# A two-layer trunk on one core: norm weight of v moved into v's stage, wider pairs, mixing over both token tiles at once

## The chip, the cores and the metric

The kernel runs on one core of a Trainium2 chip. The metric is the device time of one execution in microseconds, the median of several runs. The engines are named as in the profile: PE (TensorE, matmuls; PEld are its weight loads), DVE (VectorE), ACT (ScalarE), POOL (GpSimd) and SP (SyncE, which here issues DMAs only).

## The reference, cut to what matters

There are 256 tokens (two token tiles of 128) of width 2048 and two layers. The change touches the first layer, a gated MLP with mixing over positions, and the first projection of the second, attention.

```python
def gmlp_branch(xn, w_in, v_g, w_s, b_s, w_out):      # W = 4096
    proj = xn @ w_in                                  # [u | v | gate], 3 x 4096 columns
    uv = gelu(proj[..., :2 * W]);  zg = proj[..., 2 * W:]
    u, v = split(uv)
    v = rms_norm(v, v_g)                              # over 4096, times v_g
    vc = v.reshape(B, S // 128, 128, 16, 256)         # 16 groups of 256 columns
    mixed = einsum('gts,bnsgc->bntgc', tril(w_s), vc) + b_s
    y = u * mixed * silu(zg)
    return y @ w_out

def stick_breaking_branch(xn, w_in, w_out):
    q, k, v, zg = split(xn @ w_in, 4)                 # 4 x 2048 columns
    o = stick_breaking_attention(q, k, v) * silu(zg)
    return o @ w_out

h = x
h = h + gmlp_branch(rms_norm(h, norm_g[0]), ...)
h = h + stick_breaking_branch(rms_norm(h, norm_g[1]), ...)
return rms_norm(h, final_g)
```

All inputs are float32. All weights are streamed from memory in every execution.

## The kernel before

**Products in three terms.** A float32 tile is split into a high part (`hi`, a rounded copy that ACT makes, line 114) and the rest (`lo`, a subtraction on DVE, line 115); `cut` does this for weights, two tiles of 128x512 at a time. `terms` (lines 119 to 121) adds hi x hi, hi x lo and lo x hi in a PSUM bank. Each is one matmul of 512 columns.

**Pairs.** The class `Pair` makes two blocks of 512 output columns for both token tiles. For `ks` tile pairs (rows k and k+4 of the inner dimension, then 8 and 9 as the fifth) it uses seven products in place of eight: blocks p1 to p7 with sums and differences of the weight tiles (`minus` and the addition, DVE, lines 275 and 300; `plus`, an accumulating DMA that POOL issues, line 280) and of the left operand (`Left.sums`, and `Left.fifth` for the fifth pair of tiles, whose scratch are the buffers `sg0` and `sg1`). Every other k tile (`rest`) goes the plain way in `column(0)` and `column(1)`, one step for two k tiles, 12 matmuls. `head` makes p1 and p5, `body` p6, p2, p7, p3 and p4, then calls `mid` and makes column 0. Column 1 of a pair runs in between the blocks of the next one (`run`). A pair with `ks` = 5 has a third group of one tile in each block; where its tile is put is told by the argument `fifth`.

**Stages.** After a first plain pair, v is made in three pairs (v2, v4, v6, each with `KS_A` = 4); `evac_v` writes gelu(v) to SBUF and sums its squares. Then eight u/gate pairs (gu0 to gu7, `KS_GU` = 4), each for 512 columns of gate (column 0) and of u (column 1). Their `mid_gu` calls `mixing`: load v's norm weight (`vg`) and the mixing matrices (`ws`) on POOL's queue, mask and split `ws`, scale and split v (`vh`, `vl`), and for each token tile and group three matmuls of 256 columns (lines 580 to 582). DVE multiplies the result from PSUM by `vg` into `ym` (line 584). `evac_gu` then adds the bias and multiplies by silu(gate) (line 595, one instruction for each of the two groups) and, after u's gelu, multiplies by it (line 600). The output projection of the layer follows (pairs o0 and o2, plain products), then the first q/k pair (qk0, with `ks` = 4; the later ones, and v and gate of the attention, have 5), whose head runs beside the tail of o2.

**What sets the order.** The kernel is traced in the order of the program; small pieces of work are put in `queue` and are started by `tick`, one after so many blocks or steps. A scheduler orders the instructions of each engine by its own estimate of times; the engines then work their queues in this fixed order, with semaphores. Some orders are written out: `issue_after` puts an instruction behind another on its engine; `load` issues on SP. Buffers: three for raw weights of the plain steps (`wraw`), five for the split ones (`wspl`), one each for the tiles of the blocks.

Of the kernel before, what the change touches and what calls it, by code (L numbers as in the profile page):

```python
# [20 lines left out]
KS_GU = 4  # L21
# [8 lines left out]
def trunk_kernel(ctx: ExitStack, tc: tile.TileContext, x, xt, gcols, wst, a_w_in, a_v_norm_g,  # L30
# [188 lines left out]
    def load(out, in_):  # L219

        ins = ins_of(nc.sync.dma_start(out, in_))
        if chain:
            if chain[0] is not None:
                tc.add_manual_dep(ins, chain[0], NOSYNC, reason="order of loads")
            chain[0] = ins.name

    class Pair:
# [3 lines left out]
        def __init__(self, src, left, nk, name, ks, evac, mid=None, fifth=None):  # L231
            self.fifth = fifth or (lambda j, name: ex.tile([P, 1, CB], F32, tag=f"b1{j + 1}_2", name=name))
            self.src, self.left, self.name, self.ks = src, left, name, ks
            self.evac, self.mid = evac, mid
            self.rest = [k for k in range(nk) if k not in HALVES[0][:ks] + HALVES[1][:ks]]
            self.groups = [(k, min(2, ks - k)) for k in range(0, ks, 2)]

        def bank(self, nm):
            return ps_acc.tile([P, CB], F32, tag="acc", name=f"{self.name}_{nm}")

        def load(self, i, j):
            tiles = []
            for g, (k, n) in enumerate(self.groups):
                if i and g >= 2:
                    break
# [5 lines left out]
                load(raw, self.src(HALVES[i][k], n, j))  # L251
                tiles.append(raw)
            return tiles
# [8 lines left out]
        def block(self, b, part, acc, nm, first=False):  # L262

            for g, (k0, n) in enumerate(self.groups):
                hi, lo = cut(b[g], n, f"{self.name}_{nm}{g}")
                for kk in range(n):
                    k = k0 + kk
                    lh, ll = part(k)
                    terms(acc, lh, ll, hi[:, kk, :], lo[:, kk, :], first and k == 0, k == self.ks - 1)
                tick(1)  # L270
                yield

        def minus(self, into, b0, b1):
            for g in range(len(self.groups)):
                nc.vector.tensor_sub(into[g], b0[g], b1[g])  # L275

        def plus(self, into, i, j, g0=0):

            for g, (k, n) in list(enumerate(self.groups))[g0:]:
                adds.append(nc.gpsimd.dma_start(into[g], self.src(HALVES[i][k], n, j), accum_op=ALU.add))  # L280

        def head(self):
# [11 lines left out]
            self.minus(self.b11, self.b12, self.b11)  # L294
# [202 lines left out]
    def v_pair0(b):  # L497
        p = Pair(columns(a_w_in, W + b * CB, W + (b + 1) * CB), left, KD, f"v{b}", KS_A,
                 lambda j, t, bank: evac_v(b + j, t, bank))
        return p  # L500

# [15 lines left out]
    left.sums(max(KS_A, KS_GU), home("xs", [P, 2, 4, max(KS_A, KS_GU), P], F32R, "xs0"), "s0")  # L517
# [23 lines left out]
    l0 = ctx.enter_context(ExitStack())  # L541
    py = l0.enter_context(tc.tile_pool(name="py", bufs=1))

# [3 lines left out]
    with ExitStack() as lg:  # L547
        pa = lg.enter_context(tc.tile_pool(name="pa", bufs=1))
        pb = lg.enter_context(tc.tile_pool(name="pb", bufs=2))
        mixed = {}  # L550
        rv = None

        def mixing(b, pair):

            vg = pa.tile([P, CB], F32, tag="vg", name=f"vg{b}")
# [13 lines left out]
            mixed[b] = []  # L569
            for t in range(NT):  # L570
                vh = pb.tile([P, CB], F32R, tag="vh", name=f"vh{b}_{t}")
                vl = pb.tile([P, CB], F32R, tag="vl", name=f"vl{b}_{t}")
                vs = v_of(t, b * CB, CB)
                nc.scalar.activation(vh, vs, AF.Identity, scale=rv[:, t:t + 1])
                nc.vector.scalar_tensor_tensor(vl, vs, rv[:, t:t + 1], f(vh), op0=ALU.mult, op1=ALU.subtract)
                mp = ps_ms.tile([P, CB], F32, tag="ms", name=f"mix{b}_{t}")
                for j in range(GPB):
                    o = mp[:, j * GD:(j + 1) * GD]
                    sl = slice(j * GD, (j + 1) * GD)
                    nc.tensor.matmul(o, wh[:, j, :], vh[:, sl], start=True, stop=False)  # L580
                    nc.tensor.matmul(o, wh[:, j, :], vl[:, sl], start=False, stop=False)
                    nc.tensor.matmul(o, wl[:, j, :], vh[:, sl], start=False, stop=True)
                ym = pa.tile([P, CB], F32, tag=f"ym{t}", name=f"ym{b}_{t}")
                nc.vector.tensor_mul(ym, mp, vg)
                mixed[b].append(ym)

        def evac_gu(b, j, t, bank):
            ym = mixed[b][t]
            if j == 0:
                sg = jk.tile([P, CB], F32, tag=f"sg{t}", bufs=1, name=f"sg{b}_{t}")  # L590
                nc.scalar.activation(sg, bank, AF.Silu, scale=r1[:, t:t + 1])
                for i in range(GPB):
                    g = b * GPB + i
                    sl = slice(i * GD, (i + 1) * GD)
                    nc.vector.scalar_tensor_tensor(ym[:, sl], ym[:, sl], cols[:, NG + g:NG + g + 1], sg[:, sl],
                                                   op0=ALU.add, op1=ALU.mult)
            else:
                y = v_of(t, b * CB, CB)
                nc.scalar.activation(y, bank, AF.Gelu_apprx_tanh, scale=r1[:, t:t + 1])
                nc.vector.tensor_mul(y, y, ym)  # L600
# [11 lines left out]
        for b in range(NV):  # L612
            run(Pair(columns(a_w_in, 2 * W + b * CB, b * CB), left, KD, f"gu{b}", KS_GU,
                     lambda j, t, bank, b=b: evac_gu(b, j, t, bank), mid=lambda pair, b=b: mid_gu(b, pair)))
        flush()
        prior.clear()

# [92 lines left out]

    def o_pair(c, evac, mid):
        def fifth(j, name):

            return jk.tile([P, 1, CB], F32, tag=f"sg{j}", bufs=1, name=name)
# [67 lines left out]
    for _ in p.head():  # L782
        next(tail)
# [18 lines left out]
    nc.vector.tensor_copy(mones, scr[:, 0, :])  # L802
# [3 lines left out]
    nc.vector.tensor_copy(nu, scr2)  # L806

    never = pd.tile([P, 2, P], BF16, name="never")
    nc.vector.memset(never, 0.0)
# [3 lines left out]
    nc.vector.tensor_copy(one, ident)  # L813
# [342 lines left out]
```

## Time and profile before

| what | value |
|---|---|
| median of 3 runs (lowest, highest) | 1147.48 us (1147.37, 1147.52) |
| profiled execution: time | 1147.16 us |
| its span, from first to last instruction | 1145.4 us |
| PE busy, matmuls | 1134.8 us, 5222 |
| DVE busy | 1006.3 us |
| ACT busy | 816.6 us |
| POOL busy | 94.5 us |
| bytes moved by DMA | 263.69 MB |
| granted clock of PE | 0.998 |

The span is that of the profiled execution; the rest of its time, 1.8 us, lies around it. Times in the rows are microseconds from the span's start, lengths of single instructions in groups are ns. A row of a group gives line, engine and operation, written tile <- read tiles, shape and count, then busy time, mean length, and the idle time of the engine just before, with what ended it. Matmul records overlap, since matmuls are pipelined; the distance of their starts tells what a slot costs. DVE's and ACT's records overlap a little as well.

### The profile page before, as it was taken

How to read it: one execution, taken by the hardware profiler on the slowest of the kernel's cores; microseconds unless marked ns; L12 is line 12 of the kernel's file. 1: busy time of each engine (PE TensorE's matmuls, PEld its weight loads, DVE VectorE, ACT ScalarE, POOL GpSimd, SP SyncE). 2: the span in 40 equal slices, each digit the busy share in tenths (PEclk: the TensorE clock that was granted, in tenths of full speed). 3: DMA queues.
4: the chain of work that ended last, by engine and by line, in shares of the span. 5: the costliest groups of instructions: out<-in, count | busy, mean ns of one | idle time of the engine just before them, and what ended most of it. 6: DMA issues, size and time to landing. Idle time of an engine off the chain costs nothing.

```text
span 1145.4 us, 14888 instructions
## 1 busy us (share of the span) xinstructions
PE 1134.8 (99%) x5222; PEld 940.5 (82%) x5222; DVE 1006.3 (88%) x1108; ACT 816.6 (71%) x1072; POOL 94.5 (8%) x101
## 2 busy tenths in 40 slices
PE   9999999999999999999999999999999999999997
PEld 6788888888888888888888888888888888888885
DVE  7988888998999998987988679989889989897995
ACT  7777767767767767856657456788678877886574
POOL 0200010110110110100010000110100101100000
PEclk9999999999999999999999999999999999999999
DMA  9988787786787786677795768687787876837972
GB/s 330 319 274 250 194 262 256 195 270 231 204 258 241 212 257 224 182 236 203 254 270 171 266 201 284 170 268 208 184 283 199 211 228 173 273 87 241 334 225 82
DMA packets 135020, 263.69 MB, mean 230 GB/s; under 512 B 8864, under 2 KB 9376, under 8 KB 134816
## 3 DMA queue, kind: packets, MB, share of 16 engines
q1 hardware_dynamic: 117408, 227.57, 59.1%
q0 software_dynamic: 15728, 31.99, 15.6%
q10 hardware_dynamic: 1808, 3.17, 0.8%
q8 instruction: 41, 0.67, 0.2%
q14 instruction: 35, 0.29, 0.1%
HBM read 258.50 MB, written 4.19 MB: 229 GB/s over the span
## 4 chain that ended last, share of the span: by engine, by line
PE 96%; DMA 1%; ACT 1%; issue 1%; DVE 1%; SPq 0%; POOLq 0%; POOL 0%; ACTq 0%
PE gu_a L121 3%; PE gu_a L120 3%; PE gu_b L121 3%; PE gu_a L119 3%; PE gu_b L120 3%; PE gu_b L119 3%; PE gu_d L121 2%; PE op_acc L121 2%; PE gu_d L120 2%; PE op_acc L119 2%; PE op_acc L120 2%; PE gu_c L121 2%; PE gu_d L119 2%; PE gu_c L120 2%; PE gu_c L119 2%; PE qk_a L121 1%
## 5 line engine op out<-in xcount | busy, mean ns | idle before, releaser
L114 ACT CAST gu_p_hi<-gu_b 128x1024 fp32r<-128x1024 f32 x112 | 115.4, 1052 | 36.1 <-PE gu_c L121 19.7
L115 DVE TENSOR_TENSOR gu_p_lo<-gu_b,gu_p_hi 128x1024 fp32r<-128x1024 f32 x112 | 133.6, 1221 | 5.4 <-ACT gu_p_hi L114 4.9
L115 DVE TENSOR_TENSOR qk_p_lo<-qk_b,qk_p_hi 128x1024 fp32r<-128x1024 f32 (+1 forms) x77 | 80.8, 1075 | 8.3 <-ACT qk_p_hi L114 7.9
L114 ACT CAST gu_hi<-gu_raw 128x1024 fp32r<-128x1024 f32 x64 | 65.9, 1053 | 29.7 <-DMA gu_raw<-in_a_w_in 17.0
L115 DVE TENSOR_TENSOR gu_lo<-gu_raw,gu_hi 128x1024 fp32r<-128x1024 f32 x64 | 76.7, 1218 | 10.1 <-ACT gu_hi L114 10.1
L114 ACT CAST qk_p_hi<-qk_b 128x1024 fp32r<-128x1024 f32 (+1 forms) x77 | 70.4, 934 | 19.0 <-DMA qk_b<-in_b_w_in 4.6
L115 DVE TENSOR_TENSOR v_lo<-v_raw,v_hi 128x1024 fp32r<-128x1024 f32 (+1 forms) x41 | 48.4, 1193 | 21.2 <-ACT v_hi L114 21.0
L114 ACT CAST v_hi<-v_raw 128x1024 fp32r<-128x1024 f32 (+1 forms) x41 | 41.7, 1027 | 28.4 <-DMA v_raw<-in_a_w_in 26.3
L115 DVE TENSOR_TENSOR v_p_lo<-v_b,v_p_hi 128x1024 fp32r<-128x1024 f32 x42 | 50.2, 1220 | 3.3 <-ACT v_p_hi L114 3.1
L114 ACT CAST v_p_hi<-v_b 128x1024 fp32r<-128x1024 f32 x42 | 43.0, 1049 | 9.5 <-PE v_c L121 4.7
L115 DVE TENSOR_TENSOR bv_p_lo<-bv_b,bv_p_hi 128x1024 fp32r<-128x1024 f32 (+1 forms) x42 | 42.6, 1041 | 4.2 <-ACT bv_p_hi L114 4.0
L115 DVE TENSOR_TENSOR bg_p_lo<-bg_b,bg_p_hi 128x1024 fp32r<-128x1024 f32 (+1 forms) x42 | 42.4, 1040 | 4.1 <-ACT bg_p_hi L114 4.0
L114 ACT CAST o_p_hi<-o_b 128x1024 fp32r<-128x1024 f32 (+1 forms) x35 | 33.4, 966 | 16.6 <-PE op_acc L121 11.6
L114 ACT CAST bv_p_hi<-bv_b 128x1024 fp32r<-128x1024 f32 (+1 forms) x42 | 37.2, 908 | 9.6 <-DMA bv_b<-in_b_w_in 3.3
L114 ACT CAST bg_p_hi<-bg_b 128x1024 fp32r<-128x1024 f32 (+1 forms) x42 | 37.2, 907 | 7.9 <-DMA bg_b<-in_b_w_in 2.5
L114 ACT CAST op_hi<-op_raw 128x1024 fp32r<-128x1024 f32 x24 | 25.1, 1053 | 23.6 <-DMA op_raw<-in_a_w_out 10.5
L115 DVE TENSOR_TENSOR o_p_lo<-o_b,o_p_hi 128x1024 fp32r<-128x1024 f32 (+1 forms) x35 | 38.3, 1113 | 3.8 <-ACT o_p_hi L114 3.7
L114 ACT CAST o_hi<-o_raw 128x1024 fp32r<-128x1024 f32 x22 | 23.0, 1052 | 24.3 <-DMA o_raw<-in_a_w_out 23.2
L115 DVE TENSOR_TENSOR o_lo<-o_raw,o_hi 128x1024 fp32r<-128x1024 f32 x22 | 26.7, 1222 | 15.4 <-ACT o_hi L114 15.2
L280 POOL DMA_DIRECT2D gu_b<-in_a_w_in x16 | 19.7, 1228 | 237.7 <-DVE gu_b L275 202.2
L275 DVE TENSOR_TENSOR gu_b<-gu_b,gu_b 128x1024 f32<-128x1024 f32 x32 | 39.0, 1238 | 0.2
L114 ACT CAST qk_hi<-qk_raw 128x1024 fp32r<-128x1024 f32 x26 | 27.1, 1054 | 15.2 <-DMA qk_raw<-in_b_w_in 9.9
(773 smaller groups left out, 3820.0 us busy)
## 6 DMA issues: line engine op xcount, KB each, us to landing
gu_b<-in_a_w_in SPq DMA_DIRECT2D x64, 512.0 KB, 4.8
gu_raw<-in_a_w_in SPq DMA_DIRECT2D x64, 512.0 KB, 5.3
v_raw<-in_a_w_in SPq DMA_DIRECT2D x39, 512.0 KB, 6.0
qk_b<-in_b_w_in SPq DMA_DIRECT2D x32, 512.0 KB, 5.1
qk_raw<-in_b_w_in SPq DMA_DIRECT2D x26, 512.0 KB, 5.4
v_b<-in_a_w_in SPq DMA_DIRECT2D x24, 512.0 KB, 5.6
op_raw<-in_a_w_out SPq DMA_DIRECT2D x24, 512.0 KB, 5.4
o_raw<-in_a_w_out SPq DMA_DIRECT2D x22, 512.0 KB, 4.9
```

Of the source, the lines that this page charges most:

```text
L114: nc.scalar.copy(hi[:, sl], raw[:, sl])
L115: low[0] = nc.vector.tensor_sub(lo[:, sl], raw[:, sl], f(hi[:, sl]))
L119: nc.tensor.matmul(acc, lh, hi, start=first, stop=False, skip_group_check=True)
L120: nc.tensor.matmul(acc, lh, lo, start=False, stop=False, skip_group_check=True)
L121: nc.tensor.matmul(acc, ll, hi, start=False, stop=last, skip_group_check=True)
L275: nc.vector.tensor_sub(into[g], b0[g], b1[g])
L280: adds.append(nc.gpsimd.dma_start(into[g], self.src(HALVES[i][k], n, j), accum_op=ALU.add))
```

## The change

- Each block of 512 columns of v is multiplied by its norm weight where it lies, in the v stage, once its squares are summed: `mid_v` in pair b queues this for blocks b-2 and b-1, the first u/gate pair for the last two. The weight is loaded on POOL's queue there.
- Mixing runs over both token tiles at once: three matmuls of 512 columns for each group, in place of six of 256. ACT writes the result with the bias added back to v's place. Gate and u then each multiply it there (one DVE multiplication of 512 columns for each token tile).
- The u/gate pairs 1, 3 and 5 and the first q/k pair become five tile pairs wide. The fifth tiles of the u/gate pairs have buffers of their own (pool `exg`), those of qk0 take `sg0` and `sg1`. The fifth sums of the first layer's left operand (`x_fifth`) are made in the last v pair.
- In the u/gate pairs the head loads and uses the fifth tile ahead of the others (`fifth_first`). Loads of fifth tiles are put behind the load before them on SP's queue.
- Four small constants of the attention are made on ACT and POOL in place of DVE.

```diff
-KS_GU = 4
+KS_GU = (4, 5, 4, 5, 4, 5, 4, 4)
...
-    def load(out, in_):
+    before = [None]
+
+    def load(out, in_, behind=False):
         ins = ins_of(nc.sync.dma_start(out, in_))
+        if behind and not chain:
+            tc.add_manual_dep(ins, before[0], NOSYNC, reason="order of loads")
+        before[0] = ins.name
...
+            self.early = sorted(range(len(self.groups)), key=lambda g: (fifth_first and g < 2, g))
...
         def block(self, b, part, acc, nm, first=False):
-            for g, (k0, n) in enumerate(self.groups):
+            order = self.early if first else range(len(self.groups))
+            for g in order:
+                k0, n = self.groups[g]
...
     def v_pair0(b):
         p = Pair(columns(a_w_in, W + b * CB, W + (b + 1) * CB), left, KD, f"v{b}", KS_A,
-                 lambda j, t, bank: evac_v(b + j, t, bank))
+                 lambda j, t, bank: evac_v(b + j, t, bank), mid=lambda pair: mid_v(b, pair))
...
+    vgs = pv.enter_context(tc.tile_pool(name="pv", bufs=2))
+    def gain(b, pair):
+        vg = vgs.tile([P, CB], F32, tag="vg", name=f"vg{b}")
+        with tc.issue_after(ins_of(adds[-1])):
+            nc.gpsimd.dma_start(vg, a_v_norm_g[0:1, b * CB:(b + 1) * CB].to_broadcast([P, CB]))
+        for t in range(NT):
+            queue.append((1, lambda t=t: times(v_of(t, b * CB, CB), vg)))
+    def times(vs, vg):
+        with tc.issue_after(ins_of(low[0])):
+            nc.vector.tensor_mul(vs, vs, vg)
+    def mid_v(b, pair):
+        for i in (b - 2, b - 1):
+            gain(i, pair)
+        if b == NV - 2:
+            queue.append((1, x_fifth))
+    def x_fifth():
+        with tc.issue_after(ins_of(low[0])):
+            left.fifth(jk.tile([P, 2, 4, 1, P], F32R, tag="more", bufs=1, name="xs0e"), "s0e")
...
-                nc.gpsimd.dma_start(vg, a_v_norm_g[0:1, b * CB:(b + 1) * CB].to_broadcast([P, CB]))
                 nc.gpsimd.dma_start(ws, wst[:, b * GPB:(b + 1) * GPB, :])
...
-            mixed[b] = []
+            vh = pb.tile([P, NT, CB], F32R, tag="vh", bufs=1, name=f"vh{b}")
+            vl = pb.tile([P, NT, CB], F32R, tag="vl", bufs=1, name=f"vl{b}")
             for t in range(NT):
...
-                mp = ps_ms.tile([P, CB], F32, tag="ms", name=f"mix{b}_{t}")
-                for j in range(GPB):
-                    o = mp[:, j * GD:(j + 1) * GD]
-                    sl = slice(j * GD, (j + 1) * GD)
-                    nc.tensor.matmul(o, wh[:, j, :], vh[:, sl], start=True, stop=False)
-                    nc.tensor.matmul(o, wh[:, j, :], vl[:, sl], start=False, stop=False)
-                    nc.tensor.matmul(o, wl[:, j, :], vh[:, sl], start=False, stop=True)
-                ym = pa.tile([P, CB], F32, tag=f"ym{t}", name=f"ym{b}_{t}")
-                nc.vector.tensor_mul(ym, mp, vg)
+            for j in range(GPB):
+                sl = slice(j * GD, (j + 1) * GD)
+                mp = ps_ms.tile([P, NT, GD], F32, tag="ms", name=f"mix{b}_{j}")
+                nc.tensor.matmul(mp, wh[:, j, :], vh[:, :, sl], start=True, stop=False)
+                nc.tensor.matmul(mp, wh[:, j, :], vl[:, :, sl], start=False, stop=False)
+                nc.tensor.matmul(mp, wl[:, j, :], vh[:, :, sl], start=False, stop=True)
+                g = NG + b * GPB + j
+                nc.scalar.activation(v_of(slice(0, NT), b * CB + j * GD, GD), mp, AF.Identity, bias=cols[:, g:g + 1])

         def evac_gu(b, j, t, bank):
-            ym = mixed[b][t]
-            if j == 0:
...
+            y = v_of(t, b * CB, CB)
+            sg = jk.tile([P, CB], F32, tag=f"sg{t}", bufs=1, name=f"{'gu'[j]}{b}_{t}")
+            nc.scalar.activation(sg, bank, (AF.Silu, AF.Gelu_apprx_tanh)[j], scale=r1[:, t:t + 1])
+            nc.vector.tensor_mul(y, y, sg)
...
                 rv = rstd(1, NV, W, "nv")
+                for i in (NV - 2, NV - 1):
+                    gain(i, pair)
...
-    p = Pair(columns(b_w_in, 0, D), left1, KD, "qk0", 4, lambda j, t, bank: evac_qk(0, j, t, bank),
-             mid=lambda pair: drain())
+    p = Pair(columns(b_w_in, 0, D), left1, KD, "qk0", KS_B, lambda j, t, bank: evac_qk(0, j, t, bank),
+             mid=lambda pair: drain(), fifth=fifth)
...
-    for _ in p.head():
-        next(tail)
+    for i, _ in enumerate(p.head()):
+        if i % 3 < 2:
+            next(tail)
...
-    nc.vector.tensor_copy(mones, scr[:, 0, :])
+    nc.scalar.copy(mones, scr[:, 0, :])
```

More of the change, by code (lines that the diff above doesn't have):

```diff
@@ L250, in load @@
                     raw = self.fifth(j, name)
-                load(raw, self.src(HALVES[i][k], n, j))
-                tiles.append(raw)
-            return tiles
+                load(raw, self.src(HALVES[i][k], n, j), behind=g >= 2)
+                tiles[g] = raw
+            return [tiles[g] for g in sorted(tiles)]
         def others(self, tiles, j):
@@ L587, in evac_gu @@
-        def evac_gu(b, j, t, bank):
-            ym = mixed[b][t]
-            if j == 0:
[L590 to L600, printed above, removed]
+                nc.scalar.activation(vh[:, t], vs, AF.Identity, scale=rv[:, t:t + 1])
```

55 lines of the change are left out of this document (28 added, 27 removed).

## The prediction

> **What bounds the kernel now.** I read the page first: the engines' shares and the chain that ended last.
>
> ```profile
> PE 1134.8 (99%) x5222; PEld 940.5 (82%) x5222; DVE 1006.3 (88%) x1108; ACT 816.6 (71%) x1072; POOL 94.5 (8%) x101
> ...
> PE 96%; DMA 1%; ACT 1%; issue 1%; DVE 1%; SPq 0%; POOLq 0%; POOL 0%; ACTq 0%
> ```
>
> TensorE (PE) is busy 99% of the 1145.4 us span and makes 96% of the chain that sets the end. So the first question is how many matmuls the change takes away and what a slot costs; the second is whether another engine starves PE on the way, VectorE (DVE, 88%) first. Next come stretches from one pair to the next: a v pair, the last v pair, a u/gate pair, and the head of the first q/k pair. The columns are the busy times of PE, weight load, DVE, ACT and POOL, then clock, DMA share and GB/s.
>
> ```profile
> 98.44:139.24 40.80, 40.80 (x182) 33.80 (x180) 33.51 (x31) 28.97 (x39) 2.41 (x2) 1.00 0.78 232
> 139.24:180.04 40.80, 40.80 (x182) 33.79 (x180) 34.48 (x31) 29.09 (x39) 4.40 (x5) 1.00 0.82 242
> 222.32:264.60 42.28, 42.28 (x194) 35.23 (x192) 39.74 (x42) 30.75 (x36) 4.62 (x5) 1.00 0.77 234
> 673.60:712.50 38.90, 38.90 (x177) 32.28 (x177) 38.73 (x56) 26.93 (x36) 4.11 (x6) 1.00 0.75 231
> ```
>
> A pair four tile pairs wide has 7 x 4 x 3 = 84 matmuls in its seven products and 8 x 4 x 3 = 96 for the other eight k tiles: 180, as the weight loads of the first row say (x182 counts two that are still finishing at its edge). 40.80 / 180 = 0.2267 us a slot. The u/gate pair has 12 mixing matmuls more and takes 1.48 us more. PE has no idle in either, so in these stages time is the count of slots. DVE has 42.28 - 39.74 = 2.5 us to spare in the u/gate pair, and almost nothing (0.17 us) in the 38.9 us around the first q/k pair.
>
> **Wider pairs.** Five wide: 7 x 5 x 3 = 105, and 6 x 4 x 3 = 72 for six k tiles, together 177, three fewer. Three u/gate pairs and the first q/k pair: 12 slots x 0.2267 = **2.72 us off**. The bounds are tight, since slots of one form are removed.
>
> **Mixing.** 12 matmuls of 256 columns become 6 of 512 per pair. Now 1.48 us, then 6 x 0.2267 = 1.36: 0.12 us a pair, 8 pairs: **0.96 us off** (48 instructions fewer). Lower bound nothing, if a moving operand in two pieces of 256 gains nothing over two instructions; I take 0.96, because every 512 slot in the rows costs the same whatever feeds it.
> The Trainium skill ("TensorE: Matmul & The Clock Gate", Step-by-step) has a warm matmul take its columns at 2.4 GHz and about 2.5 ns fixed. By that, 48 fewer instructions would give 48 x 2.5 ns = 0.12 us; by the rows 0.96. The measured slot is 226.7 ns against the page's 215.8, so the measurement decides.
>
> **What DVE gains and loses in the u/gate stage.** Groups of DVE there, six pairs (222.32 to 476 us); columns: count, busy us, mean ns, idle before.
>
> ```profile
> L115 DVE TENSOR_TENSOR gu_p_lo<-gu_b,gu_p_hi 128x1024 fp32r<-128x1024 f32 x85 | 101.3, 1221 | 2.5 <-ACT gu_p_hi L114 2.2
> L275 DVE TENSOR_TENSOR gu_b<-gu_b,gu_b 128x1024 f32<-128x1024 f32 x24 | 29.2, 1235 | 0.2
> L300 DVE TENSOR_TENSOR gu_b<-gu_b,gu_b 128x1024 f32<-128x1024 f32 x12 | 14.6, 1216 | 0.0
> L595 DVE SCALAR_TENSOR_TENSOR ym<-ym,cols,sg 128x256 f32<-128x256 f32 x24 | 10.0, 479 | 0.0
> L575 DVE SCALAR_TENSOR_TENSOR vl<-v,nv_r,vh 128x512 fp32r<-128x512 f32 x12 | 8.8, 744 | 0.0
> L600 DVE TENSOR_TENSOR v<-v,ym 128x512 f32<-128x512 f32 x12 | 7.8, 689 | 2.9 <-ACT v L599 2.8
> L584 DVE TENSOR_TENSOR ym<-mix,vg 128x512 f32<-128x512 f32 x12 | 7.7, 686 | 4.9 <-PE mix L582 4.9
> L568 DVE TENSOR_TENSOR wl<-ws,wh 128x256 fp32r<-128x256 f32 x6 | 2.5, 414 | 0.0
> ```
>
> A mean is the length of one record; neighbours overlap. What one costs in a full queue is the distance of starts:
>
> ```profile
> 685.38 1.22 DVE L115 TENSOR_TENSOR o_lo<-o_raw,o_hi 128x1024 fp32r<-128x1024 f32 x1
> 686.52 1.22 DVE L300 TENSOR_TENSOR qk_b<-qk_b,qk_b 128x1024 f32<-128x1024 f32 x1
> ...
> 698.02 0.68 DVE L659 TENSOR_TENSOR h<-o_b,h 128x512 f32<-128x512 f32 x1
> 698.62 0.68 DVE L659 TENSOR_TENSOR h<-o_c,h 128x512 f32<-128x512 f32 x1
> ...
> 710.50 0.86 DVE L683 SCALAR_TENSOR_TENSOR x<-hT,cols,x 128x256 fp32r<-128x256 f32 x2
> ```
>
> 1.14 us for 1024 columns, 0.60 for 512, and 0.86 - 0.48 = 0.38 for 256. Every u/gate pair loses two ym products (-1.2) and gets four multiplications of 512 (2.4) for four scalar-tensor ones and two products (1.5 + 1.2): -1.5 us in all, and the 0.8 us a pair of waiting for the mixing. A five-wide pair adds seven single cuts less two double ones (4.2 - 2.3 = +1.9) and one tile in each of the two subtractions (+1.2): +3.1. From 39.74 it goes to 39.74 - 1.5 + 3.1 = 41.3, against PE's 177 slots and 6 of mixing, 183 x 0.2267 = 41.5. So DVE just fits, with 0.2 us left, and each wide pair is followed by a narrow one with 38.2 in 42.2 us. How far ahead DVE is at its tightest there:
>
> ```profile
> 227.76 4.62 DVE L115 TENSOR_TENSOR gu_p_lo<-gu_b,gu_p_hi 128x1024 fp32r<-128x1024 f32 x4
> ...
> 230.71 0.39 PE L120 MATMUL gu_b<-gu_p_lo,xs 128*128 128x512 f32 x1
> ```
>
> The first of the four ends at 228.98, PE takes it at 230.71: a lead of 1.7 us, which a deficit of some tenths doesn't use up. Stalls: 0 to 1 us for the three together; I take 0.3, as the rows put DVE under PE. The fifth tile, first in the head, has buffers of its own and so waits for no block of the pair before.
>
> **ACT gets the mixing's bias.** Two activations of 128x512 a pair (690 ns, as the Silu of that shape) now wait for the mixing's last matmuls, and the v split of the next pair and its casts stand behind them. ACT waits at this place already:
>
> ```profile
> L591 ACT ACTIVATE sg<-gu_a,n_r 128x512 f32<-128x512 f32 x6 | 4.1, 690 | 0.1
> ...
> 237.54 1.34 ACT L574 ACTIVATE vh<-v,nv_r 128x512 fp32r<-128x512 f32 x2 [3.09 <-PE mix L582]
> 239.74 1.06 ACT L114 CAST gu_hi<-gu_raw 128x1024 fp32r<-128x1024 f32 x1 [0.86 <-DMA gu_raw<-in_a_w_in]
> ```
>
> The split would end 1.3 us later, at about 240.2, the cast start 0.4 us later. ACT is at 30.75 of 42.28 us, so it is hidden: 0, with 0.4 us a pair (3.2 in all) if that cover were gone. Of the four constants that go from DVE to ACT and POOL, three stand between these starts, 0.4 us, in a stretch where DVE is full:
>
> ```profile
> 704.95 0.17 DVE L809 MEMSET never<- 128x128 uint32 x1
> ...
> 705.34 1.44 DVE L115 TENSOR_TENSOR qk_p_lo<-qk_b,qk_p_hi 128x1024 fp32r<-128x1024 f32 x1
> ```
>
> **The v stage.** 12 multiplications (0.60 each) in its three pairs, four more in the first u/gate pair, and once the fifth sums (8 operations of 0.28 us, as the record of one further down has it, and a 512 one: 2.8 us): up to 34.48 + 2.4 + 2.8 = 39.7 of 40.80 in the last v pair. They come behind holes such as this one:
>
> ```profile
> 118.34 1.23 DVE L115 TENSOR_TENSOR v_lo<-v_raw,v_hi 128x1024 fp32r<-128x1024 f32 x1 [5.77 <-ACT v_hi L114]
> ```
>
> With them go two loads of 256 KB a pair on POOL's queue, behind the accumulating ones:
>
> ```profile
> vg<-in_a_v_norm_g POOLq DMA_DIRECT2D x8, 256.0 KB, 8.5
> ...
> 123.51 1.20 POOL L280 DMA_DIRECT2D v_b<-in_a_w_in  x1 [36.21 <-ACT v L467]
> ```
>
> 8.5 us to landing where they are now; POOL idles 36 us between pairs, so nothing is behind them. In v4 and v6 they have 10 us and more. In v2 DMA is full:
>
> ```profile
> 40.00:60.00 20.00, 20.00 (x90) 16.57 (x89) 19.17 (x17) 15.65 (x22) 2.58 (x2) 1.00 1.05 331
> ...
> 45.83 1.20 POOL L280 DMA_DIRECT2D v_b<-in_a_w_in  x1 [0.95 <-ACT v_p_hi L114]
> ...
> 57.06 1.05 ACT L114 CAST v_p_hi<-v_b 128x1024 fp32r<-128x1024 f32 x1 [0.76 <-DMA v_b<-in_a_w_in]
> ...
> 63.89 4.63 DVE L115 TENSOR_TENSOR v_p_lo<-v_b,v_p_hi 128x1024 fp32r<-128x1024 f32 x4 [0.25 <-ACT v_p_hi L114]
> ...
> 66.03 0.39 PE L120 MATMUL v_b<-v_p_lo,xs 128*128 128x512 f32 x1
> ```
>
> 0.52 MB at 331 GB/s delay what is behind by 1.6 us; the lead there is 66.03 - 65.12 = 0.9. A stall of 0 to 0.7 us; I take 0.2, since part of the delay falls on loads that wait for a buffer anyway.
>
> **The first q/k pair** is the risky one. DVE has no gap from 673.6 to 712.5, and its lead ends at:
>
> ```profile
> 709.36 1.21 DVE L115 TENSOR_TENSOR qk_lo<-qk_raw,qk_hi 128x1024 fp32r<-128x1024 f32 x1
> ...
> 711.26 0.39 PE L120 MATMUL qk_a<-qk_lo,x 128*128 128x512 f32 x1
> ```
>
> 0.7 us. Up to there the wide pair adds seven single cuts and two subtracted tiles, 9 x 0.60 = 5.4, less 0.4 of constants: 5.0 us of DVE; and 21 slots, 4.8 us, of PE. The lead falls to 0.5. But the fifth tile goes into the buffer that the fifth sums use as scratch, and these end late:
>
> ```profile
> 680.03 0.28 DVE L170 TENSOR_TENSOR xs1e_sm<-xs1e_full,xs1e_sm 128x128 f32<-128x128 f32 x1
> ...
> qk_b<-in_b_w_in SPq DMA_DIRECT2D x12, 256.0 KB, 5.1
> ```
>
> Loaded at 680.3, landed at 685.4; then ACT and DVE. PE's third group of the first product comes two groups and two tail steps after 680, 2 x 1.36 + 2 x 2.72 = 8.2 us, at 688.2. It arrives, but a cut queued before its data is there stops DVE in a stretch where nothing is made up. 0 to 3 us; I take 0.4. SP waits with it: the tail's last load, now issued at 680.14, goes at most a microsecond later.
>
> **Sum.** -2.72 - 0.96 + 0.3 + 0.2 + 0.4 = -2.8 us. Against the profiled execution (1147.16 us, span 1145.4) 1144.4; that execution lies 0.3 under the median of the runs, 1147.48, against which it makes **1144.7 us**.
>
> **Rivals.**
> *Eaten up by stalls, chance 0.26.* The first q/k pair loses what the fifth tile waits, up to 3 us, the u/gate pairs their 1 us, v2 its 0.7: -3.7 + 4.7 = +1.0 at most; half-way 1146.2, no change to tell. For it: DVE's full stretch. Against it: PE asks for that tile 8 us after its buffer is free, and the load takes 5.
> *The mixing gives nothing, 0.05.* -2.72 + 0.9: 1145.7, no change.
> *DVE becomes the bound in the wide u/gate pairs, slower, 0.13.* If an instruction holds DVE for its whole record, a wide pair costs 20 x 1.22 + 7 x 0.69 (cuts) + 4 x 1.235 + 2 x 1.216 + 2 x 0.69 (subtractions, addition) + 4 x 0.69 + 2 x 0.744 + 2 x 0.69 + 0.41 = 44.0 us against 41.5. Three of them: 7.6 us, and 1147.5 - 3.7 + 7.6 = 1151.4. It decides from 41.5 us of DVE a pair on. For it: my own sum is 0.2 under that. Against it: starts 1.14 us apart at records of 1.22.
> The Trainium skill ("VectorE: DVE Perf Modes", The DRAIN you can't avoid) states that the next operation doesn't start until the pipe is empty, which would be this case; it adds that one not held starts earlier, and this trace shows the earlier start.
>
> **Chances.** Forecast 0.56. About 0.2%, 2.3 us, is what a measurement here tells from no change, and the forecast clears it by 0.5 only. Faster: 0.56; same: 0.26 + 0.05 = 0.31; slower: 0.13. Low end: no stall, -3.7, so 1143.8, less 0.2 for the reading; the likeliest case's own range is 1143.6 to 1145.2. The high end reaches into the stalls' worst and part of the slower case, leaving out about a tenth: 1148.3.
>
> **What would show it.** PE has 5222 - 60 = 5162 matmuls. A narrow u/gate pair takes 42.2 us and a wide one 41.5, with no PE idle; DVE's busy time in a wide pair is 41 or more. If a wide pair takes 43 or 44 with DVE full, the slower rival holds. In the first q/k head, an ACT cast or DVE cut waiting for a 256 KB load, with PE idle by 715, would show the second case. It is wrong if a stall of more than 1.5 us stands anywhere that the change touches, or if the order of an engine's queue around the v loads or the mixing has turned into a wait of PE.

## The result, and the profile after

| | before | after |
|---|---|---|
| median (lowest, highest), six runs each | 1147.21 us (1146.30, 1147.52) | 1155.92 us (1154.82, 1156.37) |
| ratio after / before, 95% interval | | 1.0076 [1.0063, 1.0089] |
| profiled execution, its span | 1147.16 us, 1145.4 us | 1155.79 us, 1154.1 us |
| PE busy, matmuls | 1134.8 us, 5222 | 1136.9 us, 5162 |
| DVE busy | 1006.3 us | 1017.1 us |
| bytes moved by DMA | 263.69 MB | 265.78 MB |

The changed kernel is 8.7 us slower; 1144.7 us was forecast, 1148.3 us was the upper end. The page of the changed kernel, its engines and its chain:

```profile
PE 1136.9 (99%) x5162; PEld 934.6 (81%) x5162; DVE 1017.1 (88%) x1125; ACT 830.3 (72%) x1112; POOL 103.9 (9%) x110
...
PE 82%; DMA 6%; DVE 6%; ACT 3%; issue 3%; SPq 0%; POOL 0%; POOLq 0%; ACTq 0%; DVEq 0%
```

The 60 matmuls are gone, exactly as counted, and the time went up. PE still shows 99% busy: a matmul's record lasts 0.39 us where the starts are 0.2267 apart, so the records cover the first part of each wait. What tells is the chain, where PE's share fell from 96% to 82% and DMA, DVE and ACT came in (a share of the chain says through whom the end was set, not how much time was lost). Next the windows of the changed kernel, with the columns of the prediction: a v pair, a round of one wide and one narrow u/gate pair, the stretch around the head of the first q/k pair, and five microseconds inside it.

```profile
98.44:139.24 40.80, 40.80 (x181) 33.81 (x180) 35.61 (x35) 28.97 (x40) 3.60 (x4) 1.00 0.83 245
348.85:434.23 85.38, 84.97 (x370) 68.89 (x369) 78.31 (x82) 64.44 (x80) 11.57 (x10) 1.00 0.79 231
672.60:720.00 47.40, 42.47 (x180) 32.21 (x179) 38.23 (x53) 27.17 (x43) 6.92 (x9) 1.00 0.62 169
685.00:690.00 5.00, 4.77 (x22) 3.61 (x20) 0.00 (x0) 0.48 (x1) 0.00 (x0) 1.00 1.10 280
```

The window around the head of the first q/k pair in the kernel before:

```profile
672.60:712.50 39.90, 39.90 (x182) 33.13 (x181) 39.73 (x56) 27.55 (x38) 4.11 (x6) 1.00 0.75 229
```

The v pair still takes 40.80 us. The round should take (177 + 6 + 180 + 6) slots x 0.2267 = 83.65 us and takes 85.38: 1.7 us lost. Before, 181 weight loads went by in 39.90 us, 0.2204 each; after, 179 need 47.40 in place of 39.46: **7.9 us lost in one place**, where 0.4 had been put down. And between 685 and 690 DVE, which had no gap at all here before, does nothing for five microseconds. PE's waits in the changed kernel (total, times, longest):

```profile
PE hT L434 <- DVE h L689: 1.5, 2, 1.4
PE qk_e L120 <- DVE qk_p_lo L115: 1.3, 1, 1.3
...
PE gu_c L120 <- DVE gu_p_lo L115: 1.0, 3, 0.4
...
PE gu_b L119 <- ACT gu_hi L114: 0.4, 1, 0.4
```

These are only the idle stretches beyond the records, so they are shorter than what was lost; they name the places. The first of them, transposes of `h` that wait for DVE's sums, lies in the same stretch, behind DVE's late cuts. How the loss in the first q/k head comes about stands in four views of the changed kernel: ACT's timeline, DVE's, POOL's, and the DMA issues between 676 and 706 us (issuing queue, count, KB each, us to landing).

```profile
680.90 1.04 ACT L114 CAST o_hi<-o_raw 128x1024 fp32r<-128x1024 f32 x1
689.52 1.57 ACT L114 CAST qk_p_hi<-qk_b 128x512 fp32r<-128x512 f32 x2 [7.58 <-DMA qk_b<-in_b_w_in]
691.00 1.04 ACT L114 CAST o_hi<-o_raw 128x1024 fp32r<-128x1024 f32 x1
...
704.88 1.57 ACT L114 CAST qk_p_hi<-qk_b 128x512 fp32r<-128x512 f32 x2 [5.58 <-DMA qk_b<-in_b_w_in]
```

```profile
680.05 0.29 DVE L170 TENSOR_TENSOR xs1e_sm<-xs1e_full,xs1e_sm 128x128 f32<-128x128 f32 x1
...
683.12 1.22 DVE L115 TENSOR_TENSOR o_lo<-o_raw,o_hi 128x1024 fp32r<-128x1024 f32 x1
690.17 0.69 DVE L115 TENSOR_TENSOR qk_p_lo<-qk_b,qk_p_hi 128x512 fp32r<-128x512 f32 x1 [5.83 <-ACT qk_p_hi L114]
...
705.53 0.69 DVE L115 TENSOR_TENSOR qk_p_lo<-qk_b,qk_p_hi 128x512 fp32r<-128x512 f32 x1 [2.33 <-ACT qk_p_hi L114]
```

```profile
679.34 1.20 POOL L294 DMA_DIRECT2D qk_b<-in_b_w_in  x1 [76.32 <-DVE xs1e_sm L168]
683.76 1.20 POOL L294 DMA_DIRECT2D qk_b<-in_b_w_in  x1 [3.23 <-DVE qk_b L286]
...
699.97 0.86 POOL L294 DMA_DIRECT2D qk_b<-in_b_w_in  x1 [6.51 <-DVE qk_p_lo L115]
```

```profile
qk_b<-in_b_w_in POOLq DMA_DIRECT2D x2, 512.0 KB, 9.8
qk_b<-in_b_w_in SPq DMA_DIRECT2D x4, 256.0 KB, 8.9
o_raw<-in_a_w_out SPq DMA_DIRECT2D x1, 512.0 KB, 6.3
qk_b<-in_b_w_in POOLq DMA_DIRECT2D x2, 256.0 KB, 4.6
```

(A row with a count can hold tiles of two widths; it shows the shape of the first.) Two holes. *The first:* the fifth sums free the buffer of block p1's fifth tile at 680.3; its 256 KB load goes out at 680.58, beside two accumulating loads of 512 KB (POOL, 679.34 and 683.76) and a 512 KB load for the tail. It takes 8.8 us (the 8.9 in the view is the median of four), and ACT's cast of it starts at 689.52. ACT's queue is in order, so its next cast for the output projection (691.00) stands behind, then DVE's cuts, then PE, which keeps running on what was ready and stops between 689 and 695. *The second:* the accumulating load that turns the tile of block p5 into that of p6 can only be issued when p5's cut has read the buffer (699.97, released by that cut), and ACT waits for it until 704.88 (5.58 us).

### The profile page after: what moved, and what is told of

The parts are those of the page before. It is cut to its first block, busy times and chain, and to the rows that moved or that the text cites. A ratio compares the mean times of both kernels' runs of the same rounds, so it can differ in the third digit from the quotient of the medians.

```text
span 1154.1 us, 14884 instructions
## 1 busy us (share of the span) xinstructions
PE 1136.9 (99%) x5162; PEld 934.6 (81%) x5162; DVE 1017.1 (88%) x1125; ACT 830.3 (72%) x1112; POOL 103.9 (9%) x110
## 2 busy tenths in 40 slices
DMA packets 136300, 265.78 MB, mean 230 GB/s; under 512 B 9120, under 2 KB 9632, under 8 KB 136096
## 4 chain that ended last, share of the span: by engine, by line
PE 82%; DMA 6%; DVE 6%; ACT 3%; issue 3%; SPq 0%; POOL 0%; POOLq 0%; ACTq 0%; DVEq 0%
DMA o_raw<-in_a_w_out 2%; PE gu_a L121 2%; PE gu_a L120 2%; PE gu_a L119 2%; PE gu_b L119 2%; PE gu_b L120 2%; PE op_acc L119 2%; PE op_acc L120 2%; PE gu_b L121 2%; PE op_acc L121 2%; PE gu_d L120 2%; PE gu_d L119 2%; PE gu_d L121 2%; PE gu_c L120 2%; PE gu_c L121 1%
## 5 line engine op out<-in xcount | busy, mean ns | idle before, releaser
L114 ACT CAST gu_p_hi<-gu_b 128x1024 fp32r<-128x1024 f32 (+1 forms) x133 | 126.1, 983 | 40.8 <-DVE gu_b L314 26.2
L115 DVE TENSOR_TENSOR gu_p_lo<-gu_b,gu_p_hi 128x1024 fp32r<-128x1024 f32 (+1 forms) x133 | 147.4, 1140 | 1.1 <-ACT gu_p_hi L114 0.2
L115 DVE TENSOR_TENSOR qk_p_lo<-qk_b,qk_p_hi 128x1024 fp32r<-128x1024 f32 (+1 forms) x84 | 85.0, 1043 | 16.1 <-ACT qk_p_hi L114 15.7
L114 ACT CAST qk_p_hi<-qk_b 128x1024 fp32r<-128x1024 f32 (+1 forms) x84 | 74.4, 906 | 30.3 <-DMA qk_b<-in_b_w_in 15.4
L115 DVE TENSOR_TENSOR gu_lo<-gu_raw,gu_hi 128x1024 fp32r<-128x1024 f32 x58 | 69.8, 1219 | 20.4 <-ACT gu_hi L114 20.3
L114 ACT CAST gu_hi<-gu_raw 128x1024 fp32r<-128x1024 f32 x58 | 60.0, 1052 | 27.0 <-DMA gu_raw<-in_a_w_in 21.4
L294 POOL DMA_DIRECT2D gu_b<-in_a_w_in x22 | 24.8, 1132 | 242.4 <-DVE gu_b L286 106.2
L286 DVE TENSOR_TENSOR gu_b<-gu_b,gu_b 128x1024 f32<-128x1024 f32 (+1 forms) x38 | 42.8, 1144 | 0.1
L120 PE MATMUL op_acc<-op_lo,yc 128*128 128x512 f32 x96 | 37.8, 394 | 0.0
```

What stands on the lines that cost most here:

```text
L114: nc.scalar.copy(hi[:, sl], raw[:, sl])
L115: low[0] = nc.vector.tensor_sub(lo[:, sl], raw[:, sl], f(hi[:, sl]))
L120: nc.tensor.matmul(acc, lh, lo, start=False, stop=False, skip_group_check=True)
```

## The experiments

The theory: the loss is made of the two holes of the first q/k pair (about 8 us) and of PE waiting for DVE's cuts in the u/gate pairs (3 to 4 us), against 3.7 us gained in slots. The rivals: the v stage or the mixing cost something; or the first q/k pair only makes up a loss that begins earlier.

**1. The first q/k pair four wide again** (`after_qk4`).

```diff
-    p = Pair(columns(b_w_in, 0, D), left1, KD, "qk0", KS_B, ..., mid=lambda pair: drain(), fifth=fifth)
+    p = Pair(columns(b_w_in, 0, D), left1, KD, "qk0", 4, ..., mid=lambda pair: drain())
-    for i, _ in enumerate(p.head()):
-        if i % 3 < 2:
-            next(tail)
+    for _ in p.head():
+        next(tail)
```

> The changed kernel with the first q/k pair four wide again (its head beside the tail as before). Theory: that pair lost 8 us of PE idle between 689 and 718 us because its fifth tiles wait for the scratch buffers of the fifth sums; without the fifth tile the idle goes and three slots come back: 1155.9 - 8.0 + 0.7 = 1148.6 us, PE idle under 1 us between 675 and 725. Rival: that stretch only collects a delay from earlier work (DVE or SP behind since the u/gate pairs); then the time stays within 2 us of 1155.9.

Measured: 1147.35 us, with the kernel before at 1147.30 beside it, 1.0001 [0.9990, 1.0012]. The edit puts the head's interleaving with the tail back too; run 6 keeps the new one and loses little, so that isn't the reason. The loss is gone, with three slots more; 1148.6 had been expected. Its window:

```profile
672.60:712.50 39.90, 39.90 (x182) 33.13 (x181) 39.02 (x52) 27.62 (x39) 5.14 (x7) 1.00 0.74 226
```

The same 181 weight loads in the same 39.90 us as before the change, so nothing earlier feeds this loss.

**2. The u/gate pairs four wide again** (`after_gu4`).

```diff
-KS_GU = (4, 5, 4, 5, 4, 5, 4, 4)
+KS_GU = (4, 4, 4, 4, 4, 4, 4, 4)
-        if b == NV - 2:
-            queue.append((1, x_fifth))
```

> The changed kernel with all u/gate pairs four wide and without the fifth sums of the first layer. Theory: the wide u/gate pairs cost 3.5 to 3.9 us of PE idle, at the places where DVE is full, and save nine slots, 2.0 us; without them 1155.9 - 1.7 = 1154.2 us, no idle over 0.2 us between 100 and 480 us. Rival: the idle comes from ACT's new wait for the mixing, not from the width; then it stays, and the nine slots make it slower, 1157.9.

Measured: 1154.69 us against 1147.30, 1.0062 [1.0046, 1.0078]. Only 1.2 us better than the whole change by the medians of two series, with nine slots (2.0 us) put back; four and six executions don't tell 1.2 us well. In its profile PE waits nowhere between 100 and 480 us, as expected, and the rival's 1157.9 is out.

**3. Both four wide again** (`after_qk4_gu4`): the two edits together; what is left of the change is the norm weight in v's stage, the mixing and the constants.

> The changed kernel with the u/gate pairs and the first q/k pair four wide: norm weight in v's stage, mixing over both token tiles, constants and load order remain. Theory: 0.96 us fewer in mixing, 0.7 us of idle in v2 by the loads of the norm weight: 1147.2 - 0.3 = 1146.9, no difference that can be told. Rival, the moves themselves cost: 1149 or more.

Measured: 1146.62 us against 1147.30, 0.9994 [0.9985, 1.0003]; in a second series (run 12) 1146.80 against 1147.58. A u/gate pair of it:

```profile
264.31:306.47 42.16, 42.16 (x187) 34.92 (x186) 37.16 (x38) 31.82 (x38) 5.53 (x4) 1.00 0.74 228
```

42.16 us where it was 42.28: the 0.12 us a pair that 12 matmuls of 256 columns save as six of 512, with DVE at 37.16 in place of 39.74. The medians are 0.7 and 0.8 lower, which neither interval sets apart from nothing; the row shows it. From this to run 1, the three wide u/gate pairs and their fifth sums cost 1147.35 - 1146.62 = 0.73 us although they take 9 x 0.2267 = 2.04 us of slots away: 2.8 us of waits.

**4. Before, with the first q/k pair alone five wide** (`before_qk5`): the reverse of edit 1 on the kernel before, with `fifth` moved out of `o_pair`.

> The kernel before with nothing changed but the first q/k pair, made five wide with its fifth tiles in the buffers of the fifth sums' scratch, head as in the changed kernel. Theory: 8.0 us of idle less three slots: 1147.2 + 7.3 = 1154.5. Rival (collected delay): within 1.5 us of 1147.2.

Measured: 1154.62 us against 1147.30, 1.0062 [1.0047, 1.0077]. This one step costs 7.3 us without any of the others; with its three slots (0.7) it loses 8.0. In the profiled execution an estimated 0.5 us of the loss is the clock: it is 0.54 between 707 and 710 us, where 12 weight loads go by with PE busy throughout, 14 in the next three microseconds at 1.00. ACT's timeline has the same two holes:

```profile
687.43 1.57 ACT L114 CAST qk_p_hi<-qk_b 128x512 fp32r<-128x512 f32 x2 [6.49 <-DMA qk_b<-in_b_w_in]
...
702.78 1.57 ACT L114 CAST qk_p_hi<-qk_b 128x512 fp32r<-128x512 f32 x2 [5.98 <-DMA qk_b<-in_b_w_in]
```

**5. The scratch of the fifth sums elsewhere** (`after_scr`), so that the fifth tiles of the first q/k pair find `sg0` and `sg1` free and can be loaded early. The rest is the whole change.

```diff
-        def fifth(self, out, name):
-            full = jk.tile([P, 2, S], F32, tag="sg0", bufs=1, ...)
-            sm = jk.tile([P, 4, P], F32, tag="sg1", bufs=1, ...)
+        def fifth(self, out, name, pool=None):
+            full = (pool or jk).tile([P, 2, S], F32, tag="sg0", bufs=1, ...)
+            sm = jk.tile([P, 4, P], F32, tag="es" if pool else "sg1", bufs=1, ...)
...
-left1.fifth(more("xs1e"), "xs1e")
+left1.fifth(more("xs1e"), "xs1e", po)
```

> The changed kernel; only the scratch of the second layer's fifth sums moves, from sg0 and sg1 to other buffers that are free then, so that the fifth tiles of the first q/k pair can be loaded early. Theory: the 3.4 us of PE idle up to 700 us go; of the 4.5 us after 700, which come from the accumulating load of the fifth tile between p5 and p6 (issued when p5's third cut is done, 5.5 us to land and be cast, for a place 4.5 us later), about 1 us stays: 1155.9 - 3.4 - 3.4 = 1149.1. Rival A, only the late buffer matters: 1148.0. Rival B, the buffer doesn't matter, DVE is simply full there: 1154 or more.

Measured: 1150.57 us against 1147.48, 1.0027 [1.0016, 1.0038]: 5.4 us better than the whole change by the medians. ACT's timeline of this kernel, then the landing of block p1's fifth tile, whose load now goes out at 641.5:

```profile
681.93 1.57 ACT L114 CAST qk_p_hi<-qk_b 128x512 fp32r<-128x512 f32 x2
...
698.89 1.57 ACT L114 CAST qk_p_hi<-qk_b 128x512 fp32r<-128x512 f32 x2 [4.33 <-DMA qk_b<-in_b_w_in]
```

```profile
qk_b<-in_b_w_in SPq DMA_DIRECT2D x1, 256.0 KB, 7.8
```

The first hole is gone: the cast comes 7.6 us earlier and waits for nothing. The load takes nearly as long as in the whole change (7.8 us), but it starts 40 us ahead of the cast. The second stays, 4.33 us on the accumulating load. It was priced too low in the expectation (1149.1), but the halves of the loss come apart as the theory has them.

**6 and 7. The fifth tile first in block p5 of the first q/k pair**, so that its accumulating load can be issued earlier; with the scratch elsewhere (`after_scr_p5`) and alone (`after_p5`).

```diff
+            if self.name == "qk0":
+                self.early = [2, 0, 1]
             self.minus(self.b11, self.b12, self.b11, self.early)
```

> As the run with the other scratch, and the second product of that pair (p5) takes its fifth tile first, so that the accumulating load starts two groups earlier. Theory: both waits gone, 1155.9 - 7.9 = 1148.0. Rival B: 1154 or more.

> The changed kernel, with p5's fifth tile first and the scratch where the change has it. Theory: the first wait stays (3.4 us before 700) and, with the fifth tile landing at 689, p5 starts later because its first group now needs the second late tile too; the accumulating load starts earlier, and the idle after 700 falls by 2 to 3 us: 1153.4. If the two waits were independent, 1151.4; if the first one makes the second, no gain: 1155.9.

Measured: 1148.71 us against 1147.48 for both edits, 1.0014 [1.0003, 1.0025]; 1153.67 us, 1.0053 [1.0032, 1.0074], for the order alone. Two windows of each, first the whole change, then the kernel with both edits, then the order alone:

```profile
680.00:700.00 20.00, 17.75 (x75) 13.53 (x74) 13.65 (x16) 9.02 (x11) 2.66 (x4) 1.00 0.65 145
700.00:720.00 20.00, 17.32 (x74) 12.54 (x74) 17.18 (x24) 13.82 (x25) 3.60 (x6) 1.00 0.66 203
```

```profile
680.00:700.00 20.00, 20.00 (x89) 16.54 (x89) 18.85 (x21) 12.12 (x17) 3.02 (x4) 1.00 0.73 158
700.00:720.00 20.00, 20.00 (x91) 15.81 (x90) 19.27 (x26) 15.24 (x25) 4.36 (x5) 1.00 0.90 314
```

```profile
680.00:700.00 20.00, 17.43 (x60) 12.98 (x60) 13.45 (x15) 7.28 (x10) 2.96 (x3) 0.83 0.83 183
700.00:720.00 20.00, 20.00 (x91) 15.86 (x90) 19.94 (x28) 18.03 (x30) 4.23 (x5) 1.00 0.69 236
```

With the order alone, the second hole closes (90 weight loads in the 20 us after 700, as with both edits, 74 in the whole change) and the first costs more (60 before 700, 74 in the whole change, 89 with both edits). One reason is that the fifth tile is now what PE asks for first in p5 as well. Another is the clock, which is low from 689 to 698 us, right behind PE's stop. Three microseconds of it:

```profile
692.00:695.00 3.00, 3.00 (x9) 2.32 (x8) 2.97 (x3) 2.82 (x4) 0.43 (x1) 0.50 0.89 123
```

PE is busy throughout, and 8 weight loads go by where 14 do at a clock of 1.00 (698 to 701). So this run doesn't price the wait alone. Each edit closes its own hole: the scratch alone gains 5.4 us, the order alone 2.2, both 7.2. Still, even the relieved wide pair is not faster than the four-wide one (1148.7 against 1147.35 of run 1, in different series): by these medians about 1.9 us of waits are left against three slots saved, 0.7 us. One place shows: between 740 and 745 us, in the pair behind, 19 weight loads go by, 23 in the kernel before.

**8. DVE relieved in the u/gate pairs** (`qk4_nomul`): run 1 without the multiplication by gelu(u). This leaves a part of the computation out.

```diff
-            nc.vector.tensor_mul(y, y, sg)
+            if j == 0:
+                nc.vector.tensor_mul(y, y, sg)
```

> The changed kernel with the first q/k pair four wide, and the multiplication by gelu(u) left out (u's activation is still made, y is not multiplied by it): 16 DVE instructions of 128x512 fewer in the u/gate stage, 1.2 us a pair. Theory (the wide u/gate pairs run DVE full in their blocks, since what it has spare in the plain steps can't be saved up): the 2.2 us of PE idle between 215 and 305 us, and what the other executions have up to 445, fall under 0.5: 1147.3 - 2 = 1145.3. Rival (ACT's wait for the mixing, or the accumulating loads of the fifth tiles): idle stays as it is, 1147.3.

Measured: 1145.37 us against 1147.48, 0.9984 [0.9974, 0.9994]. Two multiplications fewer in each of the eight pairs, 1.2 us of DVE a pair, and the kernel is 2.0 us faster than run 1 (medians of two series), about what the wide pairs were losing. PE's waits between 180 and 500 us in run 1, then in this run:

```profile
PE gu_b L119 <- ACT gu_hi L114: 0.6, 1, 0.6
PE gu_c L120 <- DVE gu_p_lo L115: 0.4, 1, 0.4
```

```profile
PE gu_d L119 <- ACT gu_d L338: 1.7, 1, 1.7
```

The waits for DVE's cuts and for the cast behind them are gone. One other wait, at 190.5 us in the first u/gate pair, is there in the profiled execution, which is 2.9 us above this kernel's median; it has nothing to do with the edit (run 11 has it too, with its cause).

**9 and 10. The same multiplication on POOL instead** (`qk4_poolmul` on run 1, `scr_p5_poolmul` on run 6). The aim was to have the relief without leaving anything out.

```diff
-            nc.vector.tensor_mul(y, y, sg)
+            (nc.gpsimd if j else nc.vector).tensor_mul(y, y, sg)
```

> The changed kernel with the first q/k pair four wide, and the multiplication by gelu(u) made on POOL in place of DVE (two of 128x512 a pair, 1.2 us of DVE). Theory (DVE full in the wide pairs' blocks): as the run without that multiplication, 1145.4, if POOL makes one in under 3 us and its accumulating loads wait no longer for it. Rival: POOL is slow or holds DVE up, so that the accumulating loads behind it start later: 1147.3 or more.

> The changed kernel with the other scratch for the fifth sums, p5's fifth tile first in the first q/k pair, and gelu(u)'s multiplication on POOL: all of the change, with its two delays taken away. If both theories hold and add up: 1155.9 - 7.2 - 2.0 = 1146.7 from the runs, and from the slots alone 1147.2 - 3.7 = 1143.5 as a floor. If the delays were one and the same, no better than 1148.7.

Measured: 1153.32 us against 1146.86, 1.0059 [1.0046, 1.0072], and 1154.42 us, 1.0065 [1.0053, 1.0077]. The theory missed both times. The rival named for the first run came: POOL holds DVE up, 1147.3 or more. In the first of the two, POOL's and DVE's timelines and PE's waits; behind them DVE in the whole change at the same place.

```profile
229.64 4.42 POOL L627 TENSOR_TENSOR v<-v,u 128x512 f32<-128x512 f32 x2 [7.82 <-ACT u L626]
249.34 1.23 POOL L294 DMA_DIRECT2D gu_b<-in_a_w_in  x1 [15.28 <-DMA gu_raw<-in_a_w_in]
```

```profile
231.10 7.52 DVE L115 TENSOR_TENSOR gu_p_lo<-gu_b,gu_p_hi 128x1024 fp32r<-128x1024 f32 x6 [0.43 <-ACT gu_p_hi L114]
```

```profile
PE gu_c L120 <- DVE gu_p_lo L115: 1.9, 4, 0.6
...
PE gu_b L120 <- DVE gu_p_lo L115: 1.2, 3, 0.4
```

```profile
231.47 5.83 DVE L115 TENSOR_TENSOR gu_p_lo<-gu_b,gu_p_hi 128x1024 fp32r<-128x1024 f32 x6
```

Two multiplications take POOL 4.42 us, and while they run six of DVE's cuts (four of 1024 columns, two of 512) take 7.52 us in place of 5.83. DVE is spared 1.2 us and loses 1.7, in the very stretch where PE waits for its cuts. The other way in which POOL could hurt, accumulating loads issued late behind the multiplications, isn't seen here: its next load comes 15.28 us later and waits for a transfer. The Trainium skill ("SBUF — State Buffer", Who interferes with whom) states that a DVE instruction with two inputs in SBUF contends with a GpSimd instruction that reads SBUF; these rows agree.

**11 and 12. Wide only from the fourth u/gate pair on** (`qk4_late`), beside run 3 once more (`qk4_gu4_again`). Edit on run 1:

```diff
-KS_GU = (4, 5, 4, 5, 4, 5, 4, 4)
+KS_GU = (4, 4, 4, 5, 4, 5, 4, 4)
```

> The changed kernel with the first q/k pair four wide and only the u/gate pairs 3 and 5 five wide. Three profiles of the same u/gate stage had their idle in its first round (215 to 305 us, 1.4 to 2.2 us); the later ones had none in one profile and 1.2 and 1.0 us in another. Theory (each wide pair is at DVE's limit, so the idle is a matter of the lead with which it starts): six slots fewer, 1.36 us, and under 1 us of idle: 0.7 to 1.8 us under the kernel before. Rival (the cost is one per wide pair, whichever): no difference to the run with all of them four wide.

> The changed kernel with all u/gate pairs and the first q/k pair four wide, once more beside the other. Theory: the mixing's 0.96 us are all that is left of the gain: 0.7 to 1.0 us under the kernel before.

Measured: 1145.43 us against 1147.58, **0.9981 [0.9973, 0.9990]**, and 1146.80 us, 0.9993 [0.9984, 1.0002]. Two wide pairs that don't wait gain 1146.80 - 1145.43 = 1.37 us; six slots are 6 x 0.2267 = 1.36. That the two agree to a hundredth is luck, with intervals about 2 us wide; the row below is the better evidence. The expectation (0.7 to 1.8 us under the kernel before) was a little low, and the rival, no difference to run 12, is unlikely. The windows of a wide and a narrow pair, and all of PE's waits between 180 and 500 us:

```profile
350.30:433.94 83.64, 83.64 (x371) 69.28 (x370) 78.03 (x82) 64.42 (x80) 11.26 (x10) 1.00 0.81 236
```

```profile
PE gu_d L119 <- ACT gu_d L338: 1.8, 1, 1.8
```

The round takes 83.64 us, the sum of its slots, where the whole change took 85.38 for the same work. The one wait is in the first u/gate pair again (190.9 us). POOL's and ACT's timelines have its cause:

```profile
186.35 3.90 POOL L97 TENSOR_TENSOR nv_r<-nv_ms,half 128x2 f32<-128x2 f32 x1 [5.33 <-DVE nv_ms L95]
```

```profile
190.28 1.33 ACT L610 ACTIVATE vh<-v,nv_r 128x512 fp32r<-128x512 f32 x2 [2.40 <-POOL nv_r L97]
```

POOL's computation of v's norm factor takes 3.90 us here and 3.89 in run 8, and 0.72 to 1.80 in the twelve other profiles, none of which has the wait. Why it takes longer in these two executions stays open. The kernel of run 11 beats both, the one before and the whole change: 2.2 us under the kernel before.

## Why the prediction was right or wrong, point by point

**Slots: right.** 5162 matmuls, and 12 slots less of 0.2267 us each: where nothing waits, runs 11 and 12 give 1.37 us for six. The bounds called tight were tight.

**Mixing: right.** 42.16 us a narrow pair, as forecast (42.2); 0.12 us a pair, 0.96 in all. The Trainium skill ("TensorE: Matmul & The Clock Gate", Step-by-step) has about 2.5 ns fixed a matmul, by which the 48 fewer instructions would have saved an estimated 0.12 us in all; the row doesn't agree, and decides. The rival in which mixing gives nothing is out.

**ACT's bias and the v multiplications: right.** The v pair keeps its 40.80 us with DVE at 35.61, and the round without waits shows ACT's part hidden. Runs 3 and 12 hold all that together with v2's stall: -0.7 and -0.8 us, where the prediction's terms (-0.96 + 0.2) make -0.76; neither is set apart from nothing, so the closeness proves little.

**The v2 stall: open.** 0.2 us was taken. PE's waits between 55 and 70 us in the whole change, and then in run 4:

```profile
PE v_c L119 <- ACT v_c L331: 0.5, 1, 0.5
```

```profile
PE v_c L119 <- ACT v_c L317: 0.3, 1, 0.3
```

Run 4 has none of the added loads in v2 and waits too, and run 2, which has them, shows no wait there. Nothing ties it to the change.

**The first q/k pair: this term sank the forecast.** The prediction had the place and the order of events: the buffer that is freed at 680.3, the load, the cut queued before its data is there. Three things in its working failed. It took 5.1 us for the landing, the median of twelve loads of that size; this one took 8.8, beside two accumulating loads of 512 KB that the trace of the kernel before shows being issued there too, with a DMA share of 1.10 and 280 GB/s between 685 and 690. It compared the landing (685.4) with PE's need (688.2, and PE did stop for it at 689.6), but in between ACT waits *in order*: the cast at the head of its queue held up a cast for the tail, whose data came in meanwhile, and DVE behind it lost 5.8 us in a stretch where it had had no gap. And it never priced the second load of a fifth tile, the accumulating one between p5 and p6, which can't be issued until p5's cut is done and holds ACT for 5.6 us more. "0 to 3 us; I take 0.4" was 8.0 (run 4). Runs 5 and 7 show the two holes one by one, run 6 both nearly closed. Why the load is slow stays open: no run took the accumulating loads away, and in run 5 the same load took 7.8 us at 641.5 with no accumulating load beside it, only loads on SP's queue (DMA share 0.89 and 300 GB/s from 641 to 650). What decides is that it goes out 40 us before its cast there.

**The wide u/gate pairs: right in what DVE costs, wrong in where it is spare.** Starts 1.14 us apart held, so the rival's 44.0 us of DVE a pair didn't come (a round of a wide and a narrow pair has 78.31, where the prediction's 41.3 and 38.2 make 79.5), nor the way to its 1151.4. But "DVE just fits, with 0.2 us left" was a sum over a pair, taken as if the spare could be used anywhere. DVE's timeline in the first wide pair:

```profile
243.95 1.23 DVE L115 TENSOR_TENSOR gu_lo<-gu_raw,gu_hi 128x1024 fp32r<-128x1024 f32 x1 [1.72 <-ACT gu_hi L114]
```

It idles 1.7 us in the plain steps, behind a cast, and 26 us later, in the blocks of the narrow pair behind, PE waits for its cuts. The term was 0.3 us; it measured 2.8 (runs 1 and 3, whose intervals reach 1 us to either side). Run 8 points to DVE's load as what decides, and run 11 shows that pairs 3 and 5 can do without the loss when pair 1 is narrow. Whether pair 1 loses by its place, behind the first u/gate pair with its four extra multiplications and its sums for rv, or because three wide pairs use up a lead that two don't, no run separates: none has pair 1 alone wide. In the profile of the whole change the later rounds lose time too (85.38), in that of run 1 they don't; what decides there from one execution to the next stays open.

**The sum.** -3.7 + 8.0 + 2.8 gives +7.1, against +8.7 measured; the first q/k pair alone measures 7.3 to 8.6 us net in its three settings (runs 1, 2 with 3, and 4), and the intervals of these runs reach 1 to 2 us to either side, so the rest isn't to be divided further.

**The rivals and the chances.** "Eaten up by stalls" named the right place and mechanism and stopped at 3 us for it, because the only bound used was the time by which the load could miss PE's need; nobody asked what ACT and DVE do meanwhile. The slower rival sat on the wrong stage. The sign to look for was right word for word: an ACT cast waiting for a 256 KB load, and PE idle before 715.

## What to carry to other kernels

Price a wider tile by the moment at which its buffer comes free and by the landing time under the loads that run *then*, and do it for each load of that tile: an engine with an ordered queue waits for the tile at its head even when everything behind it is ready. When a sum over a stage says that an engine just fits, look where in the stage its idle time lies; time that is spare in one step is of use to another only as far as the buffers let the engine run ahead. And try a widening on the late repetitions first: here the two later wide pairs by themselves gave their slots, and with the early one added the gain was more than gone.

## What was not expected of the hardware

- The 128x512 float32 multiplication takes POOL 2.2 us (4.42 for two, in the profile's record) where DVE's starts are 0.60 us apart, and DVE's subtractions beside it go from 5.83 to 7.52 us for six.
- The same 256 KB load took 8.8 us from issue to landing beside two accumulating loads of 512 KB, and 7.8 us in run 5, issued 39 us earlier beside ordinary loads. The 5.1 us of the prediction was a median of loads further on.
- In the stretch in which PE waits longest (run 7, 60 weight loads in 20 us) the granted clock is 0.83, and 0.50 in its middle; right behind the second hole, from 707 to 710, it is 0.54 in run 4 and 0.50 in run 2. In the profile of the whole change, around the same places, it is 1.00. The length of a single wait doesn't decide it: the longest distance between recorded starts behind 700 us is 1.77 us in the whole change and 1.76 in run 2. Whether the waits lower it was not tried.
